# Tokens on partitions for the head norms of block 2, one stationary for both parts of its first 16 tokens' values, and a sub-norm step of block 1 at another unit

## The chip, the cores and the metric

One Trainium2 chip, one of its cores. The metric is the time of one execution of the whole program in device microseconds; lower is better. The weights stand in device memory and are read in every execution; activations stay on chip from the input to the output.

## The reference, cut to what matters

Two stacks of two layers each run over one sequence of 512 tokens and 1024 features, in float32. In the first stack a layer is a gated feed-forward part, a mixer with three kinds of heads (band attention, differential attention with a norm of its own on the output, "sub-norm", and stick-breaking attention), and a second feed-forward part. In the second stack 16 learned tokens are put ahead, which makes 528, and a layer is a mixer and a feed-forward part with a short convolution. What the change touches is this:

```python
def head_rms_norm(y, g):                       # second stack, on the mixer's 1024 outputs
    yf = y.reshape(b, l, d // 64, 64)
    yf = yf * lax.rsqrt(jnp.mean(yf * yf, axis=-1, keepdims=True) + RMS_EPS)
    return yf.reshape(b, l, d) * g
z = jnp.einsum("bld,de->ble", u, w_in)         # q, k, v, f_logit, conv and gate parts
log_f = jax.nn.log_sigmoid(f_logit + b_forget) # 8 columns, computed with the first half of v
o = rmsnorm(o, subln_g) * (1.0 - lambda_init)  # first stack, heads of 64 of the 4 differential heads
```

## The kernel before, in words

Activations lie with features on partitions and tokens along a row. float32 matmuls are split: every operand x is held as a rounded part xh and a rest xl, every weight as wh and wl, and a product is three matmuls (mm3, lines 222 to 224), wh·xh, wh·xl and wl·xh, all added in PSUM. A token range is worked in two halves, tokens 0 to 271 and 272 to 527 in the second stack. PSUM's eight banks go by tags (line 103): acc 2, x 1, s 2, t 2, o 1. Scratch tiles of one half of the tokens share 24 buffers (the pool hp).

A mixer is written as generators that give a yield with an estimated time in ns after each small step. The class Filler (line 621) draws such steps from a queue; pipeline (line 662) walks the attention units, each in three stages (scores, transposes, values), and between the stages pumps the filler for a fixed time and calls tick, which gives the second queue, aux, 277 ns, that is one step. When the units are through, a loop pumps the filler for 1050 ns and aux for 570 ns in turn (END, line 41) until both are empty. Program order so written ranks the work; the order on each engine is then fixed when the program is built, and PE need not run what was written first.

Values of the second stack (gen_v, line 1176, with v_gen, line 768): tokens on partitions. For each block of tokens, 16, 128, 128, 128 and 128, v_gen runs over the 8 feature chunks with three matmuls each: stationary xh or xl of the block (16 or 128 columns), moving the weights (264 or 256 columns): xh·wh, xh·wl, xl·wh, lines 778 to 780. Then ACT and DVE scale by the token's norm factor and split (lines 787, 788). It runs twice per layer (g = 0 and 1), so four times in all. The call for g = 0 gives the forget logits too (forget, line 1158).

Head norms (head_norm, line 1421): called per layer for chunks [4, 5], [6, 7], [0, 1] and [2] with both halves and for chunk [3] once per half, which is 10 passes over a half per layer and 20 in all. A chunk has two heads. ACT squares the chunk (line 1437); for each half, PE sums the squares with a stationary of 2 or 4 columns (the selector selz) and the half's 272 or 256 tokens moving (line 1442); for the attention chunks, 0 to 3, PE also adds the softmax sums' squares by an identity matmul for each token block (line 1446). So mean squares lie with 2 or 4 heads on partitions and tokens along the row. ACT takes the root (line 1448), DVE the reciprocal (line 1450), ACT and DVE split it (lines 1452, 1453), and after a yield PE spreads it to 128 rows by two matmuls per chunk (line 1460), DVE multiplies (line 1464), ACT and DVE split the result for the output projection (lines 1467, 1468). All of these PSUM tiles use the one bank x. The calls for [0, 1], [2], [3] and [6, 7] go through aux, the one for [4, 5] through the filler.

The sub-norm of the first stack's mixer (subln, line 1029) has two steps. The first squares, sums with tokens on partitions (line 1037: stationary a 128x128 block of squares, moving two columns), takes root and reciprocal of a 128x16 tile (lines 1044, 1048, 1050) and widens it (line 1056). The second transposes it back (line 1063) and multiplies (lines 1066 to 1069). with_subln (line 1092) runs a step at the transposing stage of the units of the last kind that SUBLN (line 44) names, here units 1 and 2 of 12.

Of the kernel before, what the change touches and what calls it, by code (L numbers as in the profile page):

```python
# [9 lines left out]
F32 = mybir.dt.float32  # L10
F32R = mybir.dt.float32r
BF16 = mybir.dt.bfloat16
ACTF = mybir.ActivationFunctionType
ALU = mybir.AluOpType
# [3 lines left out]
KC = 8  # L18
# [4 lines left out]
HB = 272  # L23
DEPTH = 2
RMS = 1e-6
# [14 lines left out]
CT, HN = (260, 720, 617), (277, 277, 277)  # L40
END = (1050, 570)
CUT1, CUT2 = (7,), (5, 7)
OUT1, OUT2 = (5, 6, 7, 4, 3, 0, 1, 2), (0, 1, 4, 5, 2, 7, 6, 3)
SUBLN = (1, 2)
LATE = (3, 6, 7)
LAST = ("ffn3", DEPTH - 1)

# [32 lines left out]
def block_stack_kernel(ctx: ExitStack, tc: tile.TileContext, x_in, meta_in, vec_in, lam_in, wup1, wdn1, wqk1,  # L80
                       wv1, wo1, strip_a, wqk2, wv2, wcv2, wpw2, wo2, wup2, wdn2, c_ident, c_stripb,
                       c_cmask, c_fmask, c_sel, c_selc, out, n_sub=99):
    nc = tc.nc
    act, dve, pe, pool = nc.scalar, nc.vector, nc.tensor, nc.gpsimd
# [10 lines left out]
    def half(dt=F32, name="h"):  # L95
        return hp.tile([128, HB], dt, tag="h", name=name)

    small_bufs = {"mn": 8, "ls": 4, "rl": 4, "rt": 4, "rt_s": 4, "lf": 1, "lft": 1, "lfe": 1, "nl": 2, "hv": 3, "lrow": 1, "lrowb": 1, "bl": 1, "bv": 1, "br": 1, "lame": 1}

    def small(shape, name="sm"):  # L100
        return sp.tile(shape, F32, tag=name, bufs=small_bufs.get(name, 2), name=name)
# [7 lines left out]
    def bank(tag, shape=(128, 512)):  # L109
        return ps.tile(list(shape), F32, tag=tag, bufs=bank_tags[tag], name="ps_" + tag)  # L110
# [4 lines left out]
    def lbank():  # L115

        lin[0] += 1
        return bank(lin[1][lin[0] % len(lin[1])])
# [3 lines left out]
    ident = one.tile([128, 128], F32, name="ident")  # L122
# [4 lines left out]
    zeroc = one.tile([128, 1], F32, name="zeroc")  # L127
    epsc = one.tile([128, 2], F32, name="epsc")
    selz = one.tile([128, 16], F32, name="selz")
# [48 lines left out]
    def wunit(*key, back=0):  # L178

        assert plan[head[0]][0] == key, (plan[head[0]][0], key)  # L180
        head[0] += 1
        fetch(head[0] + AHEAD - back)
        return ready.pop(head[0] - 1)
# [60 lines left out]
    class Whole:  # L244

        i, n, g, c = None, TALL - T0, slice(T0, TALL), slice(0, TALL - T0)
# [883 lines left out]
    def mixer2(l, opnd, gpost, nxt):  # L1130
        H = HALF[2]
        TB = [(0, 16), (16, 144), (144, 272), (272, 400), (400, 528)]
        with ExitStack() as st:
# [21 lines left out]
            lf = {}  # L1155
# [13 lines left out]
            def log_sigmoid():  # L1169
# [3 lines left out]
                act.activation(out=e, in_=e, func=ACTF.Ln, bias=1.0)  # L1173
                dve.scalar_tensor_tensor(out=f, in0=t, scalar=0.0, in1=e, op0=ALU.min, op1=ALU.subtract)

            def gen_v(g):
                w = 264 if g == 0 else 256
                us = lambda: [wunit("mix2", l, "v", g, j) for j in range(2)]

                def get(a):  # L1180
                    tb = 0 if a == 0 else (a - 16) // 128 + 1
                    vt[g, tb] = t = mp.tile([128, 512], F32R, tag="L", bufs=26, name="v")
                    return t
                tbs = [(H[0], 0, 16, 2)] + [(h, a, b, j) for h in H for j, (a, b) in enumerate(h.tb)]
                return v_gen(opnd, us, tbs, w, get, forget if g == 0 else None)

            def vsl(h, tb):
                m = TB[tb][1] - TB[tb][0]
# [22 lines left out]
            lrow = small([128, 40], "lrow")  # L1211
# [209 lines left out]
            def head_norm(cs, hs):  # L1421

                while 2 * len(sel) < len(cs):
                    t, raw = half(F32R, "sel"), half(name="selr")
                    nc.sync.dma_start(out=raw[0:16, 0:256], in_=c_sel[:, 256 * len(sel):256 * len(sel) + 256])
                    act.activation(out=t[0:16, 0:256], in_=raw[0:16, 0:256], func=ACTF.Copy)
                    sel.append(t)
                m, attn, sqs, rr = 2 * len(cs), cs[0] < 4, {}, {}
                if attn:

                    v, lq = small([128, 20], "hv"), lrow[:, 10 * cs[0]:10 * cs[0] + 5 * m]
                    dve.scalar_tensor_tensor(out=v[:, 0:5 * m], in0=lq, scalar=64.0 * RMS, in1=lq, op0=ALU.mult,
                                             op1=ALU.mult)
                for h in hs:
                    for c in cs:
                        sqs[c, h.i] = half(name="hsq")
                        act.activation(out=sqs[c, h.i][:, h.c], in_=Y(c)[:, h.g], func=ACTF.Square)
                yield HN[0]
                for h in hs:
                    ms, r = bank("x"), half(name="hr")  # L1440
                    for i, c in enumerate(cs):
                        pe.matmul(out=ms[0:m, h.c], lhsT=selz[:, 7 - 2 * i:7 - 2 * i + m], rhs=sqs[c, h.i][:, h.c],
                                  start=i == 0, stop=not attn and c == cs[-1])
                    blocks = [(j, max(a, h.lo), b) for j, (a, b) in enumerate(TB) if h.lo <= a < h.hi]
                    for j, a, b in blocks if attn else []:
                        pe.matmul(out=ms[0:m, a - h.g0:b - h.g0], lhsT=v[:b - a, j:5 * m:5], rhs=ident[:b - a, :b - a],
                                  start=False, stop=j == blocks[-1][0])
                    act.activation(out=r[0:m, h.c], in_=ms[0:m, h.c], func=ACTF.Sqrt, scale=1.0 / 64,
                                   bias=0.0 if attn else epsc[0:m, 0:1])
                    dve.reciprocal(out=r[0:m, h.c], in_=r[0:m, h.c])  # L1450
                    rh, rl = rr[h.i] = half(F32R, "rh"), half(F32R, "rl")
                    act.activation(out=rh[0:m, h.c], in_=r[0:m, h.c], func=ACTF.Copy)
                    dve.tensor_tensor(out=rl[0:m, h.c], in0=r[0:m, h.c], in1=rh[0:m, h.c].bitcast(F32),
                                      op=ALU.subtract)
                    yield HN[1]
                for h in hs:
                    for i, c in enumerate(cs):
                        rb = bank("x")
                        for j, x in enumerate(rr[h.i]):
                            pe.matmul(out=rb[:, h.c], lhsT=sel[i // 2][0:m, i % 2 * 128:i % 2 * 128 + 128],  # L1460
                                      rhs=x[0:m, h.c], start=j == 0, stop=j == 1)
                        yield HN[2]
                        y = Y(c)
                        dve.scalar_tensor_tensor(out=y[:, h.g], in0=y[:, h.g], scalar=V("head_g_2", l, c),
                                                 in1=rb[:, h.c], op0=ALU.mult, op1=ALU.mult)
                        (yh, yl), cs_ = ytile(c, h)
                        act.activation(out=yh[:, cs_], in_=y[:, h.g], func=ACTF.Copy)
                        dve.tensor_tensor(out=yl[:, cs_], in0=y[:, h.g], in1=yh[:, cs_].bitcast(F32), op=ALU.subtract)
                        y_done.add((c, h.i))
# [60 lines left out]
            op = out_proj(2, l, ytile, gpost, nxt, OUT2, CUT2, y_done, scored)  # L1530
            fl.add("out", until_tail(op))
            us = []
# [269 lines left out]
```

## Time and profile before

| | |
|---|---|
| median of 3 runs | 3420.25 us (3419.7 to 3424.2) |
| the profiled execution's own time | 3422.85 us |
| its span, first to last instruction | 3421.1 us |
| PE busy | 3381.2 us, 21765 matmuls |
| DVE, ACT, POOL busy | 2060.9, 1524.9, 8.9 us |
| mean granted TensorE clock | 0.991 |

PE's matmuls overlap each other, so the duration of one (0.28 us for a 256-column one) is not what it adds to a run of them; what it adds is the step from one start to the next, or a piece of the chain of waits divided by its count. The stretches of the second stack's mixers are about 2070 to 2320 us and 2760 to 3015 us; the first stack's mixers run through 410 to 660 and 1430 to 1680 us.

### The profile page before, as it was taken

The page shows a single profiled execution, that of the slowest core. Times are in us where ns is not written, and L with a number is a line of the kernel's source. Part 1 is how long each engine was busy: PE and PEld are TensorE (multiplying, and loading weights), DVE is VectorE, ACT ScalarE, POOL GpSimd, SP SyncE. Part 2 cuts the span into 40 slices and gives each one's busy share as a digit, 9 for nine tenths or more (in the row PEclk, how much of TensorE's full clock was granted, in tenths as well). Part 3 has the DMA queues.
Part 4 walks back from the last instruction along what each step waited for, and adds up shares of the span by engine and source line. Part 5 has one row for each costly group of instructions (what it writes and reads, how often), then busy time and mean ns, then how long its engine had stood idle before and what let it go on. Part 6 is the DMA issues. An engine that isn't in the chain of part 4 may idle for free.

```text
span 3421.1 us, 55949 instructions
## 1 busy us (share of the span) xinstructions
PE 3381.2 (99%) x21765; PEld 2992.2 (87%) x21765; DVE 2060.9 (60%) x4433; ACT 1524.9 (45%) x3342; POOL 8.9 (0%) x28
## 2 busy tenths in 40 slices
PE   9999999999999999999999999999999999999998
PEld 8888987988888888987988898879999998799998
DVE  6442688744336442788744349768774397677743
ACT  6332566633234332566633235555443345664432
POOL 0000000000000000000000000000000000000000
PEclk9999999999999999999999999999999999999999
DMA  4223222232323223222223322102222221122222
GB/s 144 98 91 97 79 74 75 69 103 95 93 87 99 96 92 96 79 76 63 87 93 98 91 89 88 48 32 96 91 93 86 85 85 57 35 93 93 93 90 78
DMA packets 165817, 291.40 MB, mean 85 GB/s; under 512 B 19456, under 2 KB 36896, under 8 KB 165552
## 3 DMA queue, kind: packets, MB, share of 16 engines
q1 hardware_dynamic: 163648, 287.13, 26.4%
q8 instruction: 171, 2.80, 0.3%
q10 hardware_dynamic: 1904, 0.70, 0.1%
q14 instruction: 94, 0.77, 0.1%
HBM read 285.62 MB, written 2.13 MB: 84 GB/s over the span
## 4 chain that ended last, share of the span: by engine, by line
PE 88%; DVE 7%; ACT 3%; issue 1%; DMA 0%; SPq 0%; POOLq 0%; ACTq 0%; DVEq 0%
PE ps_acc L222 10%; PE ps_acc L223 10%; PE ps_acc L224 10%; PE ps_s L223 8%; PE ps_s L222 8%; PE ps_s L224 8%; PE ps_x L222 4%; PE ps_x L223 4%; PE ps_x L224 4%; PE ps_o L223 4%; PE ps_o L222 4%; PE ps_o L224 4%; PE ps_o L819 2%; PE ps_s L802 2%; DVE y L1337 1%
## 5 line engine op out<-in xcount | busy, mean ns | idle before, releaser
L200 ACT ACTIVATE wh<-wr 128x512 fp32r<-128x512 f32 (+2 forms) x1068 | 616.0, 615 | 1084.6 <-PE ps_acc L223 468.7
L201 DVE TENSOR_TENSOR wl<-wr,wh 128x512 fp32r<-128x512 f32 (+2 forms) x1068 | 693.1, 673 | 476.8 <-ACT wh L200 465.1
L222 PE MATMUL ps_acc<-xh,wh 128*128 128x256 f32 (+3 forms) x1608 | 533.5, 332 | 2.4 <-DVE qt L748 1.5
L223 PE MATMUL ps_acc<-xl,wh 128*128 128x256 f32 (+3 forms) x1608 | 521.4, 324 | 0.0
L224 PE MATMUL ps_acc<-xh,wl 128*128 128x256 f32 (+3 forms) x1608 | 521.1, 324 | 0.0
L223 PE MATMUL ps_s<-xl,wh 128*128 128x512 f32 (+3 forms) x1088 | 360.2, 331 | 2.8 <-DVE xl L283 0.8
L222 PE MATMUL ps_s<-xh,wh 128*128 128x512 f32 (+3 forms) x1088 | 357.5, 329 | 1.8 <-DVE z L531 1.6
L224 PE MATMUL ps_s<-xh,wl 128*128 128x512 f32 (+3 forms) x1088 | 356.5, 328 | 0.1
L222 PEld LDWEIGHTS ps_acc<-xh,wh 128*128 128x128 f32 x1608 | 306.4, 191 | 32.4 <-DVE qt L748 3.3
L224 PEld LDWEIGHTS ps_acc<-xh,wl 128*128 128x128 f32 x1608 | 306.0, 190 | 25.9 <-issue 1.5
L223 PEld LDWEIGHTS ps_acc<-xl,wh 128*128 128x128 f32 x1608 | 306.9, 191 | 22.1
L223 PEld LDWEIGHTS ps_s<-xl,wh 128*128 128x128 f32 x1088 | 204.8, 188 | 27.1 <-DVE xl L378 6.8
L222 PEld LDWEIGHTS ps_s<-xh,wh 128*128 128x128 f32 x1088 | 204.7, 188 | 22.2 <-DVE z L531 2.0
L224 PEld LDWEIGHTS ps_s<-xh,wl 128*128 128x128 f32 x1088 | 204.5, 188 | 18.7 <-DVE wl L201 0.3
L222 PE MATMUL ps_x<-xh,wh 128*128 128x256 f32 (+2 forms) x600 | 202.4, 337 | 0.0
L224 PE MATMUL ps_x<-xh,wl 128*128 128x256 f32 (+2 forms) x600 | 199.5, 333 | 0.0
L223 PE MATMUL ps_x<-xl,wh 128*128 128x256 f32 (+2 forms) x600 | 199.3, 332 | 0.0
L223 PE MATMUL ps_o<-xl,wh 128*128 128x512 f32 (+3 forms) x544 | 179.0, 329 | 1.0
L222 PE MATMUL ps_o<-xh,wh 128*128 128x512 f32 (+3 forms) x544 | 177.5, 326 | 0.1
L224 PE MATMUL ps_o<-xh,wl 128*128 128x512 f32 (+3 forms) x544 | 177.4, 326 | 0.0
L223 PE MATMUL ps_acc<-hl,wh 128*128 128x256 f32 (+1 forms) x528 | 168.5, 319 | 0.0
L222 PE MATMUL ps_acc<-hh,wh 128*128 128x256 f32 (+1 forms) x528 | 168.1, 318 | 0.0
(347 smaller groups left out, 7574.9 us busy)
## 6 DMA issues: line engine op xcount, KB each, us to landing
wr<-in_wup_dram SPq DMA_DIRECT2D x528, 256.0 KB, 2.8
wr<-in_wdn_dram SPq DMA_DIRECT2D x192, 256.0 KB, 2.7
wr<-in_wqk_dram SPq DMA_DIRECT2D x96, 256.0 KB, 2.8
wr<-in_wdn_dram SPq DMA_DIRECT2D x96, 192.0 KB, 2.6
wr<-in_wo_dram SPq DMA_DIRECT2D x64, 256.0 KB, 2.7
wr<-in_wv_dram SPq DMA_DIRECT2D x40, 256.0 KB, 2.9
wr<-in_wcv_dram SPq DMA_DIRECT2D x40, 256.0 KB, 2.8
dec<-fdram SPq DMA_DIRECT2D x16, 264.0 KB, 4.2
```

Of the source, the lines that this page charges most:

```text
L200: act.activation(out=hi[:, a:b], in_=raw[:, :b - a], func=ACTF.Copy)
L201: eng.tensor_tensor(out=lo[:, a:b], in0=raw[:, :b - a], in1=hi[:, a:b].bitcast(F32), op=ALU.subtract)
L222: pe.matmul(out=o, lhsT=wh[wsl], rhs=xh[xsl], start=start, stop=False)
L223: pe.matmul(out=o, lhsT=wh[wsl], rhs=xl[xsl], start=False, stop=False)
L224: pe.matmul(out=o, lhsT=wl[wsl], rhs=xh[xsl], start=False, stop=stop)
L802: pe.matmul(out=o, lhsT=a[R, qs], rhs=b[R, ks], start=j == 0, stop=j == 2 and mask is None)
L819: pe.matmul(out=o[:, q0:], lhsT=v, rhs=p[j], start=kb == 0 and j == 0, stop=kb == n - 1 and j == 1)
L1337: dve.scalar_tensor_tensor(out=y[:, s:], in0=t[0][:, :TALL - s], scalar=w[:, 30 - s:31 - s], in1=y[:, s:], op0=ALU.mult, op1=ALU.add))
```

## The change

The sub-norm's second step moves from unit 2 to unit 3. Head norms: for each token block of a half (two of 128, in the first half also one of 16) and each chunk, PE takes the block of squares as the stationary and 2 or 4 selector columns as the moving, so that mean squares lie with tokens on partitions and at most 12 columns on the row; DVE adds the softmax term or the constant, ACT takes the root and DVE the reciprocal of that small tile; after a yield, a transpose for each token block brings it to heads on partitions, in bank x, and from there the split and the rest are as before. The yield behind the split stays, so each pass over a half has one step more. Values of the first 16 tokens: POOL copies xh and xl of the tokens side by side into a tile, 48 columns for each chunk (xh, 16 zeros, xl); PE multiplies all 48 with wh and the first 16 with wl, two matmuls in place of three; ACT and DVE add rows 32 to 47 to rows 0 to 15 before the scaling.

```diff
-SUBLN = (1, 2)
+SUBLN = (1, 3)
+            def first_v(us, w, get, extra):
+                us, xm = us(), [half(F32R, "xm") for _ in range(2)]
+                for i in range(2):
+                    pool.tensor_copy(out=xm[i], in_=zeroc.to_broadcast([128, HB]))
+                    for c in range(4):
+                        for k in range(2):
+                            pool.tensor_copy(out=xm[i][:, 48 * c + 32 * k:48 * c + 32 * k + 16],
+                                             in_=opnd.at(4 * i + c)[k][:, 0:16].bitcast(F32))
+                p = lbank()
+                for c in range(KC):
+                    x = xm[c // 4][:, 48 * (c % 4):48 * (c % 4) + 48]
+                    wsl = (slice(None), slice((c % 4) * w, (c % 4 + 1) * w))
+                    wh, wl = us[c // 4]
+                    for rows, y in ((48, wh), (16, wl))[::-1 if c == KC - 1 else 1]:
+                        pe.matmul(out=p[:rows, :w], lhsT=x[:, :rows], rhs=y[wsl], start=c == 0 and rows == 48,
+                                  stop=c == KC - 1 and rows == 48)
+                    yield 2 * 109
+                t = half(name="vm")
+                act.activation(out=t[0:16, :w], in_=p[32:48, :w], func=ACTF.Copy)
+                dve.tensor_tensor(out=t[0:16, :w], in0=t[0:16, :w], in1=p[0:16, :w], op=ALU.add)
...
-                tbs = [(H[0], 0, 16, 2)] + [(h, a, b, j) for h in H for j, (a, b) in enumerate(h.tb)]
-                return v_gen(opnd, us, tbs, w, get, forget if g == 0 else None)
+                tbs = [(h, a, b, j) for h in H for j, (a, b) in enumerate(h.tb)]
+                ex = forget if g == 0 else None
+                return itertools.chain(first_v(units_of, w, get, ex), v_gen(opnd, units_of, tbs, w, get, ex))
...
-                if attn:
-
-                    v, lq = small([128, 20], "hv"), lrow[:, 10 * cs[0]:10 * cs[0] + 5 * m]
-                    dve.scalar_tensor_tensor(out=v[:, 0:5 * m], in0=lq, scalar=64.0 * RMS, in1=lq, op0=ALU.mult,
-                                             op1=ALU.mult)
...
-                    ms, r = bank("x"), half(name="hr")
-                    for i, c in enumerate(cs):
-                        pe.matmul(out=ms[0:m, h.c], lhsT=selz[:, 7 - 2 * i:7 - 2 * i + m], rhs=sqs[c, h.i][:, h.c],
-                                  start=i == 0, stop=not attn and c == cs[-1])
...
-                    for j, a, b in blocks if attn else []:
-                        pe.matmul(out=ms[0:m, a - h.g0:b - h.g0], lhsT=v[:b - a, j:5 * m:5], rhs=ident[:b - a, :b - a],
-                                  start=False, stop=j == blocks[-1][0])
-                    act.activation(out=r[0:m, h.c], in_=ms[0:m, h.c], func=ACTF.Sqrt, scale=1.0 / 64,
-                                   bias=0.0 if attn else epsc[0:m, 0:1])
-                    dve.reciprocal(out=r[0:m, h.c], in_=r[0:m, h.c])
+                    nb, ms = len(blocks), bank("x")
+                    v, r = small([128, 12], "hv")[:, :nb * m], small([128, 12], "hr")[:, :nb * m]
+                    short = blocks[0][2] - blocks[0][1]
+                    if short < 128:
+                        pool.memset(v[:, 0:m], 1.0)
+                    for k, (j, a, b) in enumerate(blocks):
+                        for i, c in enumerate(cs):
+                            pe.matmul(out=ms[:b - a, k * m:k * m + m], lhsT=sqs[c, h.i][:, a - h.g0:b - h.g0],
+                                      rhs=selz[:, 7 - 2 * i:7 - 2 * i + m], start=i == 0, stop=c == cs[-1])
+                    for k0, k1, n in ((0, 1, short), (1, nb, 128)) if short < 128 else ((0, nb, 128),):
+                        vs, mv = v[:n, k0 * m:k1 * m], ms[:n, k0 * m:k1 * m]
+                        if attn:
+
+                            j0 = blocks[k0][0]
...
+                            dve.scalar_tensor_tensor(out=vv, in0=lq, scalar=RMS, in1=lq, op0=ALU.mult, op1=ALU.mult)
+                            dve.scalar_tensor_tensor(out=vs, in0=mv, scalar=1.0 / 64, in1=vs, op0=ALU.mult,
+                                                     op1=ALU.add)
+                        else:
+                            dve.tensor_scalar(out=vs, in0=mv, scalar1=1.0 / 64, scalar2=RMS, op0=ALU.mult, op1=ALU.add)
+                    act.activation(out=v, in_=v, func=ACTF.Sqrt)
+                    dve.reciprocal(out=r, in_=v)
+                    yield HN[1]
+                    tr = bank("x")
+                    for k, (j, a, b) in enumerate(blocks):
+                        pe.transpose(tr[0:m, a - h.g0:b - h.g0], r[:b - a, k * m:k * m + m], ident[:b - a, :b - a])
+                    r = tr
```

## Rows read from the trace of the kernel before

**Rows 1.** The page, part 1: busy time, share of the span and instructions of each engine.
```profile
PE 3381.2 (99%) x21765; PEld 2992.2 (87%) x21765; DVE 2060.9 (60%) x4433; ACT 1524.9 (45%) x3342; POOL 8.9 (0%) x28
```
**Rows 2.** The page, part 4: the chain that ended last, by engine.
```profile
PE 88%; DVE 7%; ACT 3%; issue 1%; DMA 0%; SPq 0%; POOLq 0%; ACTq 0%; DVEq 0%
```
**Rows 3.** Timeline of PE, first 16 tokens' values: start us, us, engine, line, shapes (partitions*columns of the stationary).
```profile
2067.66 0.28 PE L778 MATMUL ps_o<-wh,xh 128*16 128x264 f32 x1
...
2069.10 0.28 PE L778 MATMUL ps_o<-wh,xh 128*16 128x264 f32 x1
...
2136.87 0.28 PE L780 MATMUL ps_acc<-wh,xl 128*16 128x256 f32 x1
2136.98 0.28 PE L778 MATMUL ps_acc<-wh,xh 128*128 128x256 f32 x1
```
**Rows 4.** Head norms' sums on PE: lines 1442 and 1446, then pieces of the chain.
```profile
L1442 PE MATMUL ps_x<-hsq,selz x64: 378/392/634, 2191.8 to 2990.0; 128*4 128x272 f32 x24, 128*4 128x256 f32 x24, 128*2 128x272 f32 x8, 128*2 128x256 f32 x8
L1446 PE MATMUL ps_x<-ident,hv x60: 171/272/421, 2192.8 to 2990.7; 128*2 128x128 f32 x32, 128*4 128x128 f32 x16, 16*2 16x16 f32 x8, 16*4 16x16 f32 x4
2192.86 0.67 PE ps_x L1446 x6
2193.53 0.32 PE ps_acc L222
...
2198.52 0.96 PE ps_x L1442 x4
```
**Rows 5.** Timeline around the sub-norm's sums in block 1, PE.
```profile
561.09 1.05 PE L1037 MATMUL ps_t<-selz,bsq 128*128 128x2 f32 x8
...
562.00 0.37 PE L778 MATMUL ps_x<-wh,xh 128*128 128x256 f32 x1
...
562.21 0.28 PE L779 MATMUL ps_x<-wl,xh 128*128 128x256 f32 x1
```
**Rows 6.** DVE and its like by line: ns min/median/max, first to last start, shapes.
```profile
L1450 DVE RECIPROCAL hr<-hr x20: 1736/1788/1841, 2194.9 to 2991.4; 4x272 f32<-4x272 f32 x6, 4x256 f32<-4x256 f32 x6, 2x272 f32<-2x272 f32 x4, 2x256 f32<-2x256 f32 x4
L1050 DVE RECIPROCAL br<-bv x2: 249/249/249, 566.6 to 1582.6; 128x16 f32<-128x16 f32 x2
L1044 DVE SCALAR_TENSOR_TENSOR bv<-ps_t,bl x4: 156/162/169, 564.1 to 1580.1; 128x8 f32<-128x8 f32 x4
```
**Rows 7.** Timeline at the norms of chunks 6 and 7, both layers; idle before and releaser in brackets.
```profile
2285.32 1.74 DVE L1450 RECIPROCAL hr<-hr 4x256 f32<-4x256 f32 x1
2285.34 0.39 PE L1460 MATMUL ps_x<-rh,sel 4*128 4x272 f32 x1 [0.64 <-ACT hr L1448]
...
2287.43 0.59 PE L1460 MATMUL ps_x<-rh,sel 4*128 4x272 f32 x1 [1.57 <-DVE y L1464]
...
2977.95 0.59 PE L1460 MATMUL ps_x<-rh,sel 4*128 4x272 f32 x1 [1.58 <-DVE y L1464]
```
**Rows 8.** Engines by stretch: stretch, us, busy (count) of PE, PEld, DVE, ACT, POOL; PEclk; DMA.
```profile
2287.10:2300.70 13.60, 13.10 (x49) 10.59 (x49) 4.53 (x11) 3.06 (x8) 0.00 (x0) 0.50 0.00 1
...
1580.50:1583.90 3.40, 3.40 (x14) 2.75 (x12) 2.41 (x8) 0.56 (x3) 0.00 (x0) 0.51 0.52 158
...
564.40:570.00 5.60, 5.60 (x39) 4.75 (x36) 4.68 (x16) 3.92 (x9) 0.00 (x0) 1.00 0.62 188
```
**Rows 9.** Block 1 around the sub-norm's second step: PE's wait, the stretch, chain piece.
```profile
PE ps_t L1063 <- DVE ptl L906: 1.2, 2, 0.8
...
570.00:578.00 8.00, 7.10 (x41) 5.18 (x40) 7.61 (x22) 4.93 (x15) 0.00 (x0) 1.00 0.10 36
...
577.15 0.87 PE ps_t L901 x8
```
**Rows 10.** POOL's groups by line, and the last xl of the first tokens on DVE.
```profile
L370 POOL TENSOR_TENSOR xT<-xT,f 128x256 f32<-128x256 f32 x8 | 6.3, 786 | 621.1 <-DVE f L356 614.9 <-issue 6.2
L1596 POOL TENSOR_SCALAR vec<-vec 128x8 f32<-128x8 f32 x4 | 1.0, 289 | 4.0 <-DMA vec<-in_vec_dram 4.0
...
2045.31 0.90 DVE L378 SCALAR_TENSOR_TENSOR xl<-xT,vec,xh 128x272 fp32r<-128x272 f32 x2
```

More of the change, by code (lines that the diff above doesn't have):

```diff
@@ L96, in half @@
         return hp.tile([128, HB], dt, tag="h", name=name)
-    small_bufs = {"mn": 8, "ls": 4, "rl": 4, "rt": 4, "rt_s": 4, "lf": 1, "lft": 1, "lfe": 1, "nl": 2, "hv": 3, "lrow": 1, "lrowb": 1, "bl": 1, "bv": 1, "br": 1, "lame": 1}
+    small_bufs = {"mn": 8, "ls": 4, "rl": 4, "rt": 4, "rt_s": 4, "lf": 1, "lft": 1, "lfe": 1, "nl": 2,  "lrow": 1, "lrowb": 1, "bl": 1, "bv": 1, "br": 1, "lame": 1}
     def small(shape, name="sm"):
@@ L1174, in log_sigmoid, with units_of @@
                 dve.scalar_tensor_tensor(out=f, in0=t, scalar=0.0, in1=e, op0=ALU.min, op1=ALU.subtract)
+            def first_v(us, w, get, extra):
[18 more added lines that the diff above has]
+                dve.tensor_tensor(out=t[0:16, :w], in0=t[0:16, :w], in1=p[0:16, :w], op=ALU.add)
+                r = opnd.r[0][:16, 2:3]
+                vv = get(0)[:16].rearrange("p (q a b) -> p q a b", a=2, b=64)
+                src = t[:16, 0:256].rearrange("p (q b) -> p q b", b=64)
+                act.activation(out=vv[:, :, 0, :], in_=src, func=ACTF.Copy, scale=r)
+                dve.scalar_tensor_tensor(out=vv[:, :, 1, :], in0=src, scalar=r, in1=vv[:, :, 0, :].bitcast(F32),
+                                         op0=ALU.mult, op1=ALU.subtract)
+                if extra:
+                    extra(0, 16, t, r)
             def gen_v(g):
                 w = 264 if g == 0 else 256
-                us = lambda: [wunit("mix2", l, "v", g, j) for j in range(2)]
+                made = []
+                def units_of():
+                    made[:] = made or [wunit("mix2", l, "v", g, j) for j in range(2)]
+                    return made
                 def get(a):
@@ new lines, in head_norm @@
+                    for k, (j, a, b) in enumerate(blocks):
[6 more added lines that the diff above has]
+                            j0 = blocks[k0][0]
+                            lq = lrow[:n, 10 * cs[0]:10 * cs[0] + 5 * m].rearrange("p (i t) -> p t i", t=5)[:, j0:j0 + k1 - k0]
+                            vv = vs.rearrange("p (t i) -> p t i", i=m)
+                            dve.scalar_tensor_tensor(out=vv, in0=lq, scalar=RMS, in1=lq, op0=ALU.mult, op1=ALU.mult)
[3 more added lines that the diff above has]
+                            dve.tensor_scalar(out=vs, in0=mv, scalar1=1.0 / 64, scalar2=RMS, op0=ALU.mult, op1=ALU.add)
```

## The prediction

> **What bounds the kernel now.** I read the busy time by engine first: PE is busy for 99% of the span, DVE for 60%, POOL for next to nothing [rows 1]. Then the chain that ended last: 88% of it is PE, 7% DVE, 3% ACT [rows 2]. So three things can move the time: PE work taken out or put in, a wait that PE has, and the clock at which PE runs. DVE, ACT and POOL count only where PE waits for them. For the steps I then took the timeline of the touched lines, from start to start, since a matmul of 0.28 us costs far less in a run of them [rows 3 to 5]; the durations of the DVE operations that go and of like ones that come [rows 6]; the waits at the touched places [rows 7, 9]; and the granted clock beside them [rows 8].
>
> The profiled execution took 3422.85 us, a span of 3421.1 and 1.75 around it; the median of the runs is 3420.25, that is 2.60 less. Sums are made as differences and put onto the median. About 0.2%, 6.8 us, is what a measurement of this kernel can tell from no change.
>
> **Values of the first 16 tokens.** A visit has 8 chunks of 3 matmuls now and 8 of 2 afterwards; there are 4 visits, so 32 matmuls go. Twelve starts lie in 1.44 us, 0.12 us each [rows 3], and the number of stationary columns doesn't change that: the first matmul with 128 columns behind those with 16 starts 0.11 us later [rows 3]. That gives 32 × 0.12 = **−3.8 us**. The other end: if each change between 48 and 16 columns cost the 0.09 us that PE loses behind the two-column sums of block 1 (0.21 from L778 to L779 where 0.12 is usual) [rows 5], 15 changes in 4 visits would add 5.4 and leave +1.6. I take the first, as 16 to 128 in the same loop is the nearest row.
> What is added per visit: 18 POOL copies, one ACT copy, one DVE sum. A POOL operation takes from 0.29 to 0.79 us [rows 10], so 18 make 5 to 14 us. The operands are there early: the last rest of the first half starts at 2045.31 and ends 0.90 later, and the first matmul of the visit starts at 2067.66 [rows 3, 10], 21 us of cover. It costs nothing unless the copies' two buffers come late; then the uncovered part of 14 us stands in front of PE. The weights come by the same DMAs, at the same place in SP's order, since both generators share one fetch. Behind the visit PE has the other blocks' values, so the ACT and DVE operations, under 1 us each, stop nobody.
>
> **Sums of the head norms.** Removed: 64 matmuls of L1442 at 0.96/4 = 0.24 us, 15.4 us; 60 of L1446 at 0.67/6 = 0.11 us, 6.7 us; and at the end of each of the 20 passes the next matmul takes 0.32 us where 0.12 is usual, 4.0 us [rows 4]. Together 26.1.
> Added: 32 pairs of chunk and half, each with two 128-token blocks and, as float32 takes two instructions, 128 instructions. Like ones take (562.00 − 561.09)/8 = 0.114 us [rows 5], so 14.6 us. The first half's 16-token block gives 16 pairs, 32 instructions; its rows lie nearest to the short instructions of L1446, which are inside the 0.11 us mean, so at most 0.11, and by proportion to 16 columns at least 0.014; I take 0.07, 2.2 us. Leaving such a group costs 0.09 us [rows 5], 20 times, 1.8. The 50 transposes (20 passes of 2, 10 of one more) at 0.11 [rows 4] make 5.5; leaving them costs from nothing (as 16 to 128 columns in rows 3) to the 0.20 of rows 4, and I take 0.1, 2.0. Together 26.1, net **0**, between −4 (short block at its least, leaving free) and +3.3 (short block at 0.11, leaving at 0.20).
> The Trainium skill, page "TensorE: Matmul & The Clock Gate", section "LDWEIGHTS (loading the stationary operand)", prices the load of a stationary by its columns; an estimate by it puts the short block near its lower bound, and the sum would be some 2 us less.
>
> **Waits of the head norms.** DVE's reciprocal of a row of 256 or 272 takes 1.79 us; of a 128x16 tile 0.25; the two or four small operations beside it 0.16 each [rows 6]. So DVE gets back 20 × (1.79 − 0.25 − 0.5), some 21 us, most of which PE never waited for. It did wait at chunks 6 and 7: L1460 of the second half waits 1.57 and 1.58 us for the multiplication of the first half, L1464, which stands on DVE right behind the second half's reciprocal of 1.74 (2285.32 to 2287.06), and before that 0.64 [rows 7]. With a reciprocal of 0.25 and small operations of some 0.3, about 1.2 us of each of the two waits go: **−2.4 us**. At best all goes, the 0.64 twice too: −4.4. At worst +2.6: bank x now holds for each half first the sums, then the transposes, then the spread, and the step from sums to spread grows by a PE visit, so the wait could as well stay and 1.3 be added in each layer. I take the first, because the releaser named is that very queue. The added yield makes 20 more steps on aux and filler; what was queued behind takes its place, out-projection matmuls that don't need the norms yet.
>
> **Sub-norm a unit later.** No DMA is in the step, so no queue is passed. L1063 waits 1.2 us in all for L906 [rows 9], which may go or double. DVE is full at the old place (7.61 of 8 us, PE 7.10) [rows 9], so I expect no rule by which the new one is better: **0**, between −1.2 and +1.2.
>
> Sum: −3.8 + 0 − 2.4 + 0 = **−6.2 us**, 3414.1 us; its own bounds, not all met together, are 3408 to 3420.
>
> **A second result: the clock.** Right at the wait of chunks 6 and 7, PE runs 13.6 us at half its clock, 2287.1 to 2300.7 at 0.50 (1.2 in place of 2.4 GHz); that is a loss of 6.8 us, and the second layer has the same wait [rows 7, 8]. My sum leaves it in place. Shorter half-clock stretches follow other thin PE work: after the second layer's sums with two columns 3.4 us at 0.51, after the same group in the first layer none, 1.00 [rows 8]. So such a group may cost 1.7 us, and need not.
> The eight transposes of L901 run in 0.87 us in a stretch at 1.00 [rows 9]. The Trainium skill, page "TensorE: Matmul & The Clock Gate", section "Part 4: PE-mode transpose", says transposes don't count as PE activity as other matmuls do; this speaks against 50 added ones, and that stretch doesn't bear it out.
>
> **Rivals.**
> A, the forecast: the sum alone, clock as before, 3414.1.
> B: with the wait shortened, the 13.6 us at 0.50 go too, in one layer (3414.1 − 6.8 = 3407.3) or both (3400.5). For it: the stretch begins with the wait. Against: one stretch in rows 8 came with no long wait, so the wait need not be the cause, and a third of it stays.
> C: the savings are eaten: the change of 48 and 16 columns drains (+5.4), or the wait moves from DVE's reciprocal to the bank x: 3418 to 3422, and the change in the number of instructions does not become time.
> D, slower: the sums and transposes, 20 groups with two to four moving or four stationary columns, let the clock fall behind many of them. Price 1.7 us a group; from (6.2 + 6.8)/1.7, about 8 groups, it is slower by over 0.2%; ten make 3431. For it: one of the two like groups had it. Against: the old sums have few columns too, and the new ones are shorter.
>
> **How the numbers follow.** A 0.42, B 0.30 (0.18 one layer, 0.12 both), C 0.18, D 0.10. A's bounds stand on both sides of 3413.4, where faster by 0.2% begins: 0.20 faster, 0.22 same. B is faster, C the same; D 0.08 slower, 0.02 the same. Faster 0.50, same 0.42, slower 0.08. The range reaches from B with both layers to past C, 3401 to 3424, and leaves out D and a little of B.
>
> **What would show it.** Right: a visit has 16 matmuls, 0.11 to 0.13 us apart; a pass's sums take about 0.114 us an instruction; L1450's successor takes about 0.25 us; the second L1460 at chunks 6 and 7 waits under 0.5 us. B: the granted clock is 1.00 behind it. Wrong: starts of 0.2 us in a visit (C), POOL as releaser of a visit's first matmul, a wait at the transposes, or new stretches near 0.5 behind the norms (D).

## The result, and the profile of the changed kernel

| | before | after |
|---|---|---|
| median | 3419.97 us (3418.53 to 3424.2, 4 runs) | 3454.99 us (3451.93 to 3458.87, 4 runs) |
| ratio | | 1.0101, 95% interval 1.0085 to 1.0117 |
| span of the profiled execution | 3421.1 us | 3450.0 us |
| mean granted TensorE clock | 0.991 | 0.985 |

The changed kernel is 35 us slower. The forecast was 3414.1 us, and its range ended at 3424.

The page of the changed kernel, part 1, to be read beside [rows 1]:

```profile
PE 3406.8 (99%) x21819; PEld 3019.8 (88%) x21819; DVE 2038.8 (59%) x4477; ACT 1528.8 (44%) x3350; POOL 39.6 (1%) x110
```

PE has 54 instructions more, as counted (96 more for the sums, 60 fewer of L1446, 50 transposes, 32 fewer for the values), DVE got back 22 us, POOL is busy for 31 us more. Nothing here explains 35 us: PE is as full as before and only busy for longer.

Two views show where the time went. First the engines by stretch. The columns are those of [rows 8]; the first row is in the first stack, where the change touches nothing but the sub-norm, the next two are the second stack's mixers. The kernel before:

```profile
60.00:330.00 270.00, 270.00 (x1172) 219.73 (x1171) 110.29 (x178) 82.24 (x152) 0.00 (x0) 1.00 0.30 95
...
2060.00:2325.00 265.00, 256.68 (x1836) 221.57 (x1835) 195.69 (x472) 144.51 (x361) 0.47 (x3) 0.95 0.19 62
2750.00:3015.00 265.00, 256.72 (x1843) 221.75 (x1843) 196.56 (x474) 147.83 (x365) 0.20 (x1) 0.95 0.19 62
```

The changed kernel, with the stretch behind the norms of chunks 6 and 7 as the last row:

```profile
60.00:330.00 270.00, 270.00 (x1161) 217.76 (x1160) 109.14 (x177) 81.65 (x151) 0.00 (x0) 1.00 0.30 94
...
2065.00:2340.00 275.00, 265.44 (x1848) 234.52 (x1848) 189.37 (x512) 149.70 (x372) 15.89 (x38) 0.91 0.18 56
2750.00:3030.00 280.00, 269.53 (x1924) 238.91 (x1923) 201.68 (x544) 155.23 (x387) 13.77 (x41) 0.93 0.19 58
...
2304.90:2325.40 20.50, 19.07 (x74) 16.25 (x74) 5.84 (x17) 4.05 (x12) 0.23 (x2) 0.50 0.00 1
```

In the first stack the same matmuls, of 512 moving columns, at full clock and without a gap, start every 270/1172 = 0.2304 us before and every 270/1161 = 0.2326 us after: 1% slower in code that nobody touched. In the mixers the granted clock fell from 0.95 to 0.91 and 0.93; by 1 − clock times length, an estimate, that is 27 us lost before and 44 after. The stretch at half clock behind the norms of chunks 6 and 7 is 20.5 us long, where it was 13.6 [rows 8].

A landmark for the drift in the first stack is the sub-norm's sum on DVE, L1044, whose first and last start lie a layer apart. The line of the changed kernel:

```profile
L1044 DVE SCALAR_TENSOR_TENSOR bv<-ps_t,bl x4: 156/162/168, 568.1 to 1592.5; 128x8 f32<-128x8 f32 x4
```

The distance is 1024.4 us; before it was 1580.1 − 564.1 = 1016.0 [rows 6].

Second, PE's waits in the second stack's first mixer: engine, what it waited for, us in total, times, longest. The kernel before, 2060 to 2325 us:

```profile
PE ps_x L1460 <- DVE y L1464: 1.6, 1, 1.6
...
PE ps_acc L222 <- DVE y L1313: 0.3, 1, 0.3
```

The changed kernel, 2073 to 2350 us:

```profile
PE ps_acc L222 <- DVE y L1348: 3.3, 2, 3.1
PE ps_x L1509 <- DVE rl L1502: 1.8, 1, 1.8
PE ps_x L1479 <- DVE rl L1502: 0.9, 1, 0.9
```

L1348 is L1313 of before, the step of the filler that empties a PSUM bank of a projection; a wait of 0.3 became 3.1 us. L1509 and L1479 are the norms' spread and sums.

The chain of waits of the changed kernel shows what stands ahead of that 3.1 us wait (start, us, what):

```profile
2183.50 0.65 DVE y L1372
2184.15 0.47 DVE pt L1343
2184.62 0.65 DVE y L1372
2185.46 0.65 DVE y L1372
2186.11 0.47 DVE pt L1343
2186.58 0.64 DVE y L1372
2187.22 0.34 DVE y L1348
2187.61 0.39 PE ps_acc L222
```

DVE works through taps of the long convolution (L1372), which another queue hands out, and PE stands until L1348, 0.34 us long, has had its turn.

### The profile page after: what moved, and what is told of

Same layout as the page of the kernel before. It is cut to its first block, busy times and chain, and to the rows that moved or that the text cites. A ratio compares the mean times of both kernels' runs of the same rounds, so it can differ in the third digit from the quotient of the medians.

```text
span 3450.0 us, 56247 instructions
## 1 busy us (share of the span) xinstructions
PE 3406.8 (99%) x21819; PEld 3019.8 (88%) x21819; DVE 2038.8 (59%) x4477; ACT 1528.8 (44%) x3350; POOL 39.6 (1%) x110
## 4 chain that ended last, share of the span: by engine, by line
PE 89%; DVE 7%; ACT 3%; issue 1%; DMA 0%; POOLq 0%; SPq 0%; ACTq 0%; DVEq 0%
PE ps_acc L222 10%; PE ps_acc L224 10%; PE ps_acc L223 10%; PE ps_s L223 8%; PE ps_s L222 8%; PE ps_s L224 8%; PE ps_x L222 4%; PE ps_x L224 4%; PE ps_x L223 4%; PE ps_o L223 4%; PE ps_o L222 4%; PE ps_o L224 4%; PE ps_s L802 2%; PE ps_o L819 2%; DVE y L1372 1%
```

## The experiments

All runs stand beside runs of the kernel before on the same chip, so parts are compared by their ratios; the medians of two rows can come from different chips. A ratio of 1.0010 is 3.4 us. The last column is an estimate of the time that half clock took: the median over the executions of time × (1 − mean granted clock). For the kernel before it is 24 us beside every row, for the changed kernel 55; the clock is given to 0.001, which is 3.4 us.

| run | what it is | median us | ratio (95%) | half clock, us |
|---|---|---|---|---|
| shift_before | before, tiles 32 bytes on | 3430.62 | 1.0027 (1.0019 to 1.0036) | 27 |
| shift64 | before, tiles 64 bytes on | 3422.11 | 1.0009 (1.0000 to 1.0018) | 24 |
| same_place | before, tiles where the changed kernel has them | 3435.71 | 1.0048 (1.0035 to 1.0062) | 31 |
| align_after | changed, tiles put back | 3441.91 | 1.0052 (1.0038 to 1.0065) | 59 |
| first_only | first 16 tokens' values alone | 3438.45 | 1.0041 (1.0029 to 1.0054) | 34 |
| pace_only | before, announced times alone | 3431.83 | 1.0037 (1.0025 to 1.0049) | 33 |
| first_old_pace | values alone, old announced times | 3425.91 | 1.0017 (1.0008 to 1.0027) | 27 |
| copies_only | before, POOL's copies beside it | 3420.63 | 1.0002 (0.9992 to 1.0011) | 24 |
| align_old_pace | changed, tiles put back, old announced times | 3426.74 | 1.0016 (1.0007 to 1.0025) | 43 |
| norms_only | head norms alone | 3422.63 | 1.0001 (0.9992 to 1.0010) | 38 |
| subln_only | sub-norm alone | 3420.17 | 1.0000 (0.9990 to 1.0009) | 24 |
| norms_subln | head norms and sub-norm | 3420.22 | 1.0000 (0.9991 to 1.0009) | 36 |
| norms_wide | head norms with a wide transpose | 3409.08 | 0.9967 (0.9955 to 0.9980) | 31 |

### The place of the tiles

The diff also changes the list of scratch buffers: three of 20 columns go (hv), two of 12 with that name and two of 12 (hr) come. In the memory plan a small buffer takes a multiple of 32 bytes a row, so 3 × 96 became 4 × 64 bytes, and every large operand tile that is laid out behind them moved 32 bytes back. Four kernels test that; three have a new buffer that is never used, and the fourth has the old buffers in another number and size.

shift_before and align_after, the same edit to the kernel before and to the changed one:

```diff
-"nl": 2
+"nl": 3
```

> The kernel before with one unused small scratch buffer more, 32 bytes a row; no instruction differs, but all large operand tiles behind it lie 32 bytes further on, at odd multiples of 32 bytes, as they do in the changed kernel (before: multiples of 64). Theory P (place): matmuls with 512 moving columns start every 233 ns in place of 231 in the first stack, the drift of about 12 us that the changed kernel shows there, where nothing of it was changed: 3420 + 12 = 3432 us, between 3428 and 3436. Rival Q (the drift belongs to that execution or that chip, not to the program): 3420, within 4 us.

> The changed kernel with the same unused buffer, which puts its large tiles back on multiples of 64 bytes. Theory P: 12 us less than the changed kernel, 3443 us (3438 to 3447), the drift outside the mixers gone, the half-clock stretches as they were. Rival Q: 3455. Rival R (the place also decides the half-clock stretches in block 2): below 3430.

The landmark L1044 in the run shift_before:

```profile
L1044 DVE SCALAR_TENSOR_TENSOR bv<-ps_t,bl x4: 155/162/168, 564.5 to 1585.6; 128x8 f32<-128x8 f32 x4
```

and in the run align_after:

```profile
L1044 DVE SCALAR_TENSOR_TENSOR bv<-ps_t,bl x4: 156/164/168, 564.4 to 1580.4; 128x8 f32<-128x8 f32 x4
```

The distance is 1021.1 us with the kernel before moved and 1016.0 with the changed kernel put back, that of the kernel before. Q falls: the place costs by itself. But 5.1 us more at the landmark and a ratio of 1.0027 are less than the changed kernel's 8.4 us and the 1.0101 − 1.0052 = 0.0049 that align_after won. R falls too: align_after has 3441.91 us, not below 3430.

Nor is the loss of shift_before where theory P put it. Its stretches:

```profile
60.00:330.00 270.00, 270.00 (x1173) 219.86 (x1172) 110.28 (x178) 82.28 (x152) 0.00 (x0) 1.00 0.30 95
1100.00:1290.00 190.00, 190.00 (x816) 152.98 (x815) 83.73 (x133) 57.30 (x100) 0.00 (x0) 1.00 0.29 94
```

and the later one in the kernel before:

```profile
1100.00:1290.00 190.00, 190.00 (x823) 154.27 (x823) 84.03 (x134) 58.86 (x105) 0.00 (x0) 1.00 0.30 94
```

The first stretch runs as in the kernel before, where P expected 233 ns a start; the later one has 816 matmuls in place of 823. So which stretch pays differs with the offset too.

shift64, with a count of 4 in that place, asks whether multiples of 64 are what matters.

> The kernel before with two unused small buffers more, 64 bytes a row: the large tiles move twice as far as in the run that moved them by 32, but lie on multiples of 64 again; no instruction differs. Theory P64 (what costs is lying off the multiples of 64): 3420 us, within 4, and the units of the first stack at the times of before. Rival (any move of these tiles against the other ones costs): 3428 or more.

```profile
L1044 DVE SCALAR_TENSOR_TENSOR bv<-ps_t,bl x4: 155/162/168, 565.9 to 1583.0; 128x8 f32<-128x8 f32 x4
```

1017.1 us and a ratio of 1.0009 whose interval begins at 1.0000: nearly nothing. The landmark can't tell it from no change, since runs with the tiles unmoved have from 1015.7 (norms_subln) to 1017.9 us (copies_only).

same_place has the tiles of the kernel before at the changed kernel's own addresses:

```diff
-"hv": 3
+"hv": 2
...
-                    v, lq = small([128, 20], "hv"), lrow[:, 10 * cs[0]:10 * cs[0] + 5 * m]
+                    v, lq = small([128, 32], "hv"), lrow[:, 10 * cs[0]:10 * cs[0] + 5 * m]
```

> The kernel before, whose scratch tiles for the softmax terms are two of 32 columns in place of three of 20: every instruction and its order are those of before, but the large tiles lie 32 bytes earlier, at the very addresses that they have in the changed kernel. Theory P (the place of the tiles, as an effect of its own that differs from one place to the next): the sums of the sub-norm in the two layers of the first stack lie 1024 us apart as in the changed kernel, 1016 in the kernel before, and the time is 13 to 17 us longer, 3433 to 3437. Rival (the place gives some 9 us wherever it is off the multiples of 64, and the rest of the changed kernel's loss in the first stack is another effect): 1021 us apart, 3427 to 3431.

Its landmark:

```profile
L1044 DVE SCALAR_TENSOR_TENSOR bv<-ps_t,bl x4: 156/162/166, 567.6 to 1590.6; 128x8 f32<-128x8 f32 x4
```

and its engines by stretch:

```profile
60.00:330.00 270.00, 270.00 (x1162) 217.76 (x1161) 109.18 (x177) 81.95 (x152) 0.00 (x0) 1.00 0.29 94
```

1023.0 us, 1162 matmuls where the changed kernel had 1161, and 1.0048, some 16 us. That is the changed kernel's drift, with no matmul and no order changed. So the place is some 16 us of the 35 by the ratios (14 by the medians of the changed kernel and align_after, each less that of before beside it), and its price differs from one offset to another. Which operand of the matmuls, or which engine's access beside them, feels the offset was not tried.

### The values of the first 16 tokens

first_only is the kernel before with first_v and the new gen_v, as in the diff of the change.

> The kernel before with the first 16 tokens' values of the changed one alone; large tiles on multiples of 64. Theory F (32 matmuls fewer at 0.12 us, POOL hidden): 3416 us, 3413 to 3419. Rival (48 to 16 columns drains, or POOL's copies are late): 3420 to 3426. Rival (its visits start a half-clock stretch): 3422 or more, with a new stretch near 0.5 behind a visit.

It is 14 us slower by its ratio: theory F falls. The price of a matmul is not the reason. In the timeline of the changed kernel a visit's starts step by 0.12 to 0.13 us, so 48 and 16 columns in turn drain nothing:

```profile
2082.66 0.29 PE L1191 MATMUL ps_o<-wl,xm 128*16 128x264 f32 x1
2082.79 0.28 PE L1191 MATMUL ps_o<-wh,xm 128*48 128x264 f32 x1
2082.91 0.28 PE L1191 MATMUL ps_o<-wl,xm 128*16 128x264 f32 x1
2083.03 0.28 PE L1191 MATMUL ps_o<-wh,xm 128*48 128x264 f32 x1
```

But the waits of first_only, 2060 to 2330 us, begin with the one that the changed kernel has:

```profile
PE ps_acc L222 <- DVE y L1348: 3.3, 2, 3.1
PE ps_acc L222 <- DVE qt L748: 2.1, 2, 1.9
```

Two things can put it there: the time that a step of the generator announces to the filler (218 ns now, 327 before), which moves everything that is written behind it; or POOL's copies and the buffers that they hold. pace_only changes the first alone:

```diff
-                yield 3 * 109
+                yield (2 if n == 16 else 3) * 109
```

> The kernel before, whose 8 steps of a visit's first 16 tokens are announced to the filler with 218 ns each in place of 327, as in the changed kernel; the instructions are those of before, only their order in the second stack's mixers shifts. Theory G (the new values cost their 18 us through the announced times: every unit behind them meets other filler work): 3432 to 3440 us, with a PE wait of about 3 us on DVE's y at a matmul of L222 as in the run with the new values alone. Rival H (the cost is POOL's copies and the buffers that they take): 3420, within 4.

Its waits, 2060 to 2330 us:

```profile
PE ps_acc L222 <- DVE y L1313: 3.3, 2, 3.1
PE ps_acc L222 <- DVE qt L748: 2.1, 2, 1.9
```

The same two waits to the tenth, and 1.0037, with the matmuls and DVE operations of the kernel before; the median is just under the range of theory G. copies_only does the second alone, ahead of the old matmuls:

```diff
+                def copies():
+                    xm = [half(F32R, "xm") for _ in range(2)]
...
+                    yield from v_gen(opnd, us, tbs, w, get, forget if g == 0 else None)
```

> The kernel before with POOL's 18 copies of a visit and their two buffers beside it, their result unused and the 24 matmuls of a visit as before. Theory G: 3420, within 4. Rival H: 3430 or more, from the two scratch buffers that each visit takes out of 24, or from POOL's copies beside DVE.

1.0002: POOL's copies cost nothing, as forecast. H falls. Then the announced time put back, in the values alone and in the whole change:

```diff
-                    yield 2 * 109
+                    yield 3 * 109
```

> The new values alone, each of the 8 steps announced with 327 ns as in the kernel before. Theory G: the added waits and half-clock stretches go, and the 32 matmuls that were saved show: 3416 us, 3413 to 3421. Rival H: 3434 to 3440, as with 218 ns.

> The changed kernel with its large tiles on multiples of 64 and the 8 steps of a visit announced with 327 ns in place of 218; the instructions are those of the changed kernel. Theory G (announced times): some 12 us less than the 3442 of the run with the tiles put back, 3430, between 3425 and 3435, and the PE wait of 3.1 us on DVE's y gone. Rival (beside the new norms the order is another one, and the announced times don't matter): 3438 to 3446.

align_old_pace comes to 3426.74 us, 15 us under align_after by the medians and 12 by the ratios, with the same instructions and tiles. The long wait is gone (2060 to 2340 us):

```profile
PE ps_acc L222 <- DVE y L1348: 0.3, 1, 0.3
```

and with it most of the added half-clock time. Engines by stretch of align_after:

```profile
2065.00:2340.00 275.00, 265.75 (x1861) 236.38 (x1861) 181.21 (x485) 145.13 (x360) 13.21 (x26) 0.91 0.19 60
2750.00:3030.00 280.00, 269.97 (x1891) 239.43 (x1890) 193.22 (x520) 151.25 (x375) 13.42 (x41) 0.91 0.19 60
```

and of align_old_pace:

```profile
2065.00:2340.00 275.00, 266.54 (x1932) 237.79 (x1932) 187.59 (x505) 149.46 (x375) 13.80 (x26) 0.94 0.20 62
2750.00:3030.00 280.00, 271.22 (x2007) 242.90 (x2006) 196.65 (x529) 156.86 (x397) 9.09 (x23) 0.95 0.20 62
```

0.91 against 0.94 and 0.95 over 275 and 280 us is 8 and 11 us at full clock, of 21 between the two profiled executions; over all executions the table has 59 against 43. So within the change announced times alone move the order, the order brings waits, and PE at half clock takes most of what is lost. That it is the waits that let the clock fall is not shown. In the changed kernel half clock stands right behind the wait of 3.1 us, which ends at 2187.6:

```profile
2188.90:2195.70 6.80, 6.80 (x42) 6.38 (x41) 3.11 (x19) 3.64 (x14) 0.00 (x0) 0.50 0.51 157
```

In the profiled execution of pace_only the same wait ends at 2173.4, and the clock is 1.00 from 2160 to 2205 us. That execution (3428.38 us, below the median of 3431.83) has no more half clock in the mixers than the kernel before; PE is busy 6 us less in them. Over all executions of pace_only half clock is 33 us against 24. The kernel before, then pace_only:

```profile
2065.00:2340.00 275.00, 266.68 (x1917) 231.38 (x1917) 201.03 (x486) 150.44 (x376) 0.47 (x3) 0.96 0.19 63
2750.00:3030.00 280.00, 271.72 (x1968) 236.57 (x1967) 207.29 (x503) 157.52 (x390) 0.20 (x1) 0.96 0.19 62
```

```profile
2065.00:2340.00 275.00, 263.95 (x1892) 228.97 (x1892) 198.77 (x480) 145.62 (x366) 0.41 (x3) 0.96 0.19 62
2750.00:3030.00 280.00, 268.33 (x1931) 232.34 (x1932) 204.37 (x497) 150.19 (x379) 0.20 (x1) 0.96 0.18 60
```

Theory G holds for the whole change and half for the values alone: with the old announcement these are still at 1.0017, 6 us, not the 4 us faster that the 32 saved matmuls would make. Part of the rest is the third rival of first_only: in first_old_pace, as in first_only, the second visit runs at half clock, where the kernel before has 1.00 from 2130 to 2141 us. The row of first_old_pace:

```profile
2137.30:2140.70 3.40, 3.40 (x19) 2.72 (x18) 3.40 (x10) 1.28 (x4) 0.00 (x0) 0.51 0.03 11
```

The fourth visit has 0.60 from 2831.0 to 2834.4 us, so the two cost 3 us. What else there is stays open; the order on PE differs too, as the visit's matmuls now stand behind the first 128 tokens' instead of ahead of them.

### The head norms and the sub-norm

subln_only is the first line of the diff, norms_only the new head_norm, norms_subln both; the last two have one unused small buffer so that the tiles stay in place.

> The kernel before with the sub-norm's second step at unit 3 alone. In the changed kernel the first layer's mixer lost 1.8 us around it and the second's won 1.6. Theory S0 (no net effect): 3420, within 4. Rival (the step adds a half-clock stretch in each layer): 3424 to 3430; the parts measured so far, 10 of place, 18 of values and 2 of norms, leave 5 of the 35 us to it.

> The kernel before with the head norms of the changed one alone; large tiles on multiples of 64. Theory C (the new norms are what brings the added half-clock stretches, some 20 us, and saves about 3 us of work): 3437 us, 3430 to 3445, with PE waiting at the sums of the second half for the split of the first half's transposes, and 20 us near 0.5 behind that in each layer. Rival (the norms cost nothing, the stretches come with the other parts): 3414 to 3422.

> The changed kernel without the new values, the large tiles on multiples of 64: new norms and the sub-norm at unit 3. If the parts simply add: 3420 + 2 + 1 = 3423 us, 3419 to 3427, so that the place (10 to 13 us) and the values (18) make up the rest of the 35. Rival (norms and sub-norm together bring the 4 us that the sum of the parts lacks): 3428 or more.

All three are within 0.1% of before. For norms_only theory C said 3437 us, and it falls: the norms alone don't make the kernel slower. But no change of time is here not the same as no effect. Half clock takes 38 us in norms_only and 36 in norms_subln, against 24 before: the new norms cost 12 to 14 us of clock and win as much elsewhere. The stretches of norms_only, to be read beside those of the kernel before above:

```profile
2065.00:2340.00 275.00, 268.61 (x1969) 239.87 (x1968) 189.16 (x509) 150.04 (x378) 0.98 (x8) 0.94 0.20 63
2750.00:3030.00 280.00, 273.49 (x2012) 244.31 (x2011) 194.31 (x524) 154.64 (x390) 0.61 (x5) 0.94 0.19 62
```

In these executions the clock takes 11 us more and PE stands idle 4 us less; where the rest is won was not traced. The wait and the stretch that theory C named are there. In the timeline of the changed kernel the second half's sums (L1479) stand behind the split of the first half's transposes (L1498), since both use the one bank x (idle before and releaser in brackets):

```profile
2304.44 0.48 PE L1498 MATMUL ps_x<-ident,hr 16*4 16x16 f32 x3 [0.44 <-DVE hr L1494]
2305.87 1.45 PE L1479 MATMUL ps_x<-selz,hsq 128*128 128x4 f32 x6 [0.94 <-DVE rl L1502]
```

The waits of norms_only, 2060 to 2335 us:

```profile
PE ps_x L1444 <- DVE rl L1467: 1.1, 2, 0.9
...
PE ps_x L1474 <- ACT rt_s L328: 0.9, 1, 0.9
PE ps_x L1474 <- DVE y L1368: 0.9, 1, 0.9
```

So the old wait of 1.6 us behind the long reciprocal was exchanged for others on the same bank. norms_wide takes that away: the transposes leave the middle, DVE widens the reciprocals to 64 columns a head, and one transpose for each chunk and token block does the work of small transposes, split and spread.

```diff
-                    tr = bank("x")
...
-                        pe.transpose(tr[0:m, a - h.g0:b - h.g0], r[:b - a, k * m:k * m + m], ident[:b - a, :b - a])
+                        t = half(name="hR")
+                        dve.tensor_copy(out=t[:b - a, 0:64 * m].rearrange("p (i b) -> p i b", i=m),
+                                        in_=r[:b - a, k * m:k * m + m].unsqueeze(2).to_broadcast([b - a, m, 64]))
...
-                            pe.matmul(out=rb[:, h.c], lhsT=sel[i // 2][0:m, i % 2 * 128:i % 2 * 128 + 128],
-                                      rhs=x[0:m, h.c], start=j == 0, stop=j == 1)
+                            pe.transpose(rb[:, a - h.g0:b - h.g0], t[:b - a, 128 * i:128 * i + 128],
+                                         ident[:b - a, :b - a])
```

> The new head norms alone, the large tiles on multiples of 64, and with another way back to tokens along the row: DVE widens the reciprocals of a token block to 64 columns a head (as the sub-norm of block 1 does), and a transpose for each chunk and token block gives the 128 rows directly; the small transposes, their split and the 64 spreading matmuls of L1460 fall away, and bank x holds no transposes between the two halves' sums. The sums are float32 without a split, so nothing is lost. Theory B (PE's work at the norms and the waits for the one bank are what is left to win): the 64 spreads, some 0.33 us each with the row changes, 21 us, against 80 transposes at 0.11, 9 us: 12 us less than before, 3408, between 3400 and 3413, and the stretch at half clock behind the norms of chunks 6 and 7 shorter than the 17 to 20 us of the run with the new norms alone. Rival (DVE's widening, five operations of 0.3 to 0.5 us in a call for two halves, takes over the waits, or the order shifts against it): 3417 to 3424.

0.9967, 11 us faster than the kernel before: theory B holds for the time. Its page, part 1, and, from its waits (2060 to 2325 us), the only one left at the norms (L1466 is the wide transpose, L1470 the multiplication):

```profile
PE 3370.5 (99%) x21817; PEld 3000.9 (88%) x21817; DVE 2034.7 (60%) x4503; ACT 1511.7 (44%) x3318; POOL 10.3 (0%) x38
```

```profile
PE ps_x L1466 <- DVE y L1470: 0.5, 1, 0.5
```

PE is busy for 10.7 us less than before [rows 1], and DVE, in spite of the widening, for 26 less. The half-clock stretch at chunks 6 and 7 is gone (1.00 from 2260 to 2340 us), but one stands earlier, 2200 to 2217 us at 0.58, and half clock takes 31 us over all executions against 24. So the time is won in work and waits, not in clock; the run doesn't tell the two apart. Of the kernels here it is the fastest, and it has one of the three parts of the change, in another form. Nothing was combined with it.

## Why the prediction was wrong

**The values, −3.8 us: the step that failed.** The price of a matmul, 0.12 us, and "It costs nothing" of POOL's copies were right (timeline of L1191, copies_only). What failed is that the working stopped at instructions. The new generator announces 218 ns a step where the old one announced 327; I counted yields for the norms but not what each step announces, and took it that "PE has the other blocks' values" behind the visit and that no one else would notice. The filler and the convolution's taps go by these times. The part costs 14 us by its ratio, and pace_only alone makes 13: a PE wait of 3.1 us where 0.3 stood in the first mixer, and 33 us at half clock in place of 24.

**A term that was not there: the place.** Nothing in my sum stood for the edit in the list of small buffers. It was put at nothing without a reason. same_place prices it at 16 us, nearly half of the loss, in stretches that I had read as untouched.

**The clock, left as it was.** The sum kept the half-clock time [rows 8]. In the changed kernel it is 55 us over all executions against 24; by the runs the norms bring 14 of that and win it back elsewhere, and the announced times some 16.

**The sums, 0 us.** The steps were right. In the changed kernel twelve instructions, four of them with a stationary of 16 columns, start at

```profile
2210.98 1.24 PE L1479 MATMUL ps_x<-selz,hsq 128*16 128x4 f32 x12
```

and the next matmul at 2212.08: 1.10 us, where 0.114 and 0.07 each would make 1.19. But that norms_only is at 1.0001, near the forecast for the norms, is luck: the sum held the clock as it was, and the run lost 14 us more to it (38 against 24) and won as much that the sum did not have.

**The waits, −2.4 us.** DVE's reciprocal did shrink to 0.19 us in the median (forecast 0.25) and DVE got its 22 us (forecast 21), and the second spread at chunks 6 and 7 no longer waits 1.57 us for a reciprocal. But the bank x keeps PE waiting for the split instead. At the norms' lines PE waits 3.1 and 3.4 us in the two mixers of the changed kernel, 2.2 and 3.0 before, so 1.3 us more and not 2.4 less. That was the mechanism of the upper end of my bounds, and I chose the other one because the old row named the old releaser. The median reciprocal of the changed kernel:

```profile
L1494 DVE RECIPROCAL hr<-hv x20: 163/192/228, 2215.1 to 3019.9; 128x12 f32<-128x12 f32 x6, 128x8 f32<-128x8 f32 x6, 128x6 f32<-128x6 f32 x4, 128x4 f32<-128x4 f32 x4
```

**The sub-norm, 0 us.** Right: 1.0000.

**The rivals.** D had the sign and the form, half-clock stretches, and half of the cause. It priced a group of the norms' thin instructions at 1.7 us and needed some 8 of them, 14 us, to be clearly slower; norms_only has all 20 groups and 14 us more half clock, but wins them back. What makes the whole change slow are the place and the stretches that the announced times add, 59 against 43 us. The Trainium skill, page "TensorE: Matmul & The Clock Gate", section "Part 4: PE-mode transpose", says that transposes don't count as PE activity in the same way, which speaks for D. norms_only with 50 transposes and norms_wide with 80 lose 38 and 31 us to half clock, the kernel before 24; no run parts the transposes from what else changed, so the rule is neither shown nor refuted here. B's condition never came about: the wait was exchanged, not shortened. C's doubt about 48 and 16 columns is refuted by the timeline; its other half, the wait that moves to the bank x, came true.

The parts add up: some 16 us of place, 14 of values, none of norms and sub-norm make 30 of 35; the rest is within the intervals of the ratios. Taken back one after the other, the tiles bring the changed kernel from 1.0101 to 1.0052 and the announced times from there to 1.0016.

## What to carry to other kernels

In a kernel whose order is paced by announced times, a cheaper step is also a shorter announcement: change the work and the announcement in separate runs, and price the second by looking for what is queued on the other engines at the places to which things move. When an edit adds or drops a scratch buffer, compare the addresses of the large tiles before and after, and put them back with an unused buffer, before judging the edit. A faster operation behind a single shared bank only helps if the bank is held for less time; take a use of the bank away, as norms_wide does. Read the time lost to half clock beside the time itself: a part that measures as nothing can be a saving and a loss of the same size.

## What the runs showed of the hardware

The rate of a run of 512-column matmuls depends on where the tiles lie in a partition: 0.2304 us a start at the place of before and 0.2324 (270/1162) 32 bytes earlier, the same instructions in the same order, at full granted clock and without gaps. 32 bytes further on the same stretch has 0.2302 (270/1173), but a later one 0.2328 (190/816) where the place of before has 0.2309 (190/823). Over one layer of the first stack that made 1016.0 us at the first place, 1021.1 us 32 bytes on and 1023.0 us 32 bytes back; the 1017.1 us 64 bytes on lie within what runs with unmoved tiles show. Putting the changed kernel's tiles back gave 1016.0 us again.
